# One DMA queue in order of need for the first loads, and the second layer's modulation weights moved into the first feed-forward stage

## The chip, the cores and the metric

The kernel is one program on all 8 cores of one Trainium2 chip. Each core computes one half of one of four sequences. The metric is the device time of the slowest core, in microseconds (us).

A run lists each core's span and the mean clock that TensorE (PE in the profile) was granted. Most executions agree within 0.3%, but in some of them, whatever the kernel, the cores of one die (0 to 3 or 4 to 7) or of both get a lower clock and take some per cent longer: these are slow runs. One die was also often at a lower clock than the other in runs that still count as fast, which moves the slowest core by up to 30 us. So beside the verdict of the fast runs I give, for each kernel, its **undisturbed time**: the median span over the four cores of a die, and of these the median over the dies that ran at that kernel's best clock. It is a time of middling cores, so it is lower than the time of the slowest core, and it is only compared with other undisturbed times of the same chip, unless said.

## The reference, cut to what matters

Two layers; each has a mixing sub-layer (one projection feeds a gated convolution, a spatial gate and a pooling) and a feed-forward sub-layer. Both are scaled and shifted by a modulation that is computed from a conditioning vector:

```python
for l in range(DEPTH):                                   # DEPTH = 2, D_MODEL = 1024
    ada = (c_act @ w_ada[l] + b_ada[l])[:, None, :]      # w_ada[l]: 1024 x 6144
    sh1, sc1, gt1, sh2, sc2, gt2 = jnp.split(ada, 6, axis=-1)
    h = x * (1.0 + sc1) + sh1
    z = h @ w_in[l] + b_in[l]                            # branches b, c, x, u, v, p, gates
    ...                                                  # mixers A, B, C, gates, merge, w_o
    x = layer_norm(ALPHA * x + gt1 * (merged @ w_o[l]), ...)
    h = x * (1.0 + sc2) + sh2
    up_a, up_g = jnp.split(h @ w_up[l] + b_up[l], 2, axis=-1)
    f = gelu(causal_dwconv(up_a, ...) + ...) * up_g
    x = layer_norm(ALPHA * x + gt2 * (f @ w_down[l]), ...)
```

So nothing of layer 0 can start before the first third of its modulation and x are there, and the modulation of layer 1 is not needed before layer 1.

## The kernel before

The program is recorded as a list of operations; a list scheduler with a cost model then fixes the order on every engine when the kernel is built. Weights are float32 in memory and are cast to bfloat16 on the way in, by DMAs of the GpSimd queue. They land in a pool of buffers chosen at recording time (`wget` takes one, `wput` gives it back). A core handles its 2240 tokens in two passes, each of three pieces.

Modulation weights, 512 output columns at a time, are "wada": 2.1 MB read, 32 matmuls with one column. Twelve of them make a layer.

```python
def load_x(a, b, base, dst=None, after=()):
    dst = xT[:, :, xc(base, a, b)] if dst is None else dst
    dma("sp", dst, xs[:, :, a:b], writes=[dst], nbytes=..., after=after)

def ada_step(l, g, reg=REG_W):
    h, w = wget(wada_d[l, g], 4 * UNIT, reg=reg)
    ...
    group([(P[:, jj:jj + 1], wv[:, k, jj * 128:(jj + 1) * 128], cact[:, k:k + 1], ...) for jj in range(4) for k in range(8)])
    wput(h)

def tick(n=1):                       # the next modulation step of the to-do list
    for _ in range(n):
        if todo:
            todo.pop(0)()
```

The start, and the to-do list (8 steps of layer 0, then the 12 of layer 1):

```python
load_x(*x_in[0], 0)
for g in range(4):
    ada_step(0, g, (REG_B, REG_C)[g // 2])
    if g == 2:
        hold = [R.last["pe"]]
der_mix(0)
make_h0(*x_in[0], 0)
for xp in x_in[1:]:
    load_x(*xp, 0, after=hold)
    make_h0(*xp, 0)
load_x(0, XOFF, 0, dst=stage, after=hold)
...
for g in range(4, 12):
    todo.append(must(lambda g=g: ada_step(0, g, REG_B)))
for g in range(12):
    todo.append(lambda g=g: ada_step(1, g))
```

The mixing sub-layer: eight units of mixer A (`mix_a`: three projections of 8 matmuls, so 24 matmuls for each of three token pieces), the v blocks of the spatial gate, the u part, bands, eight merges. The bias rows bcv and bsb are its side loads.

```python
def side_loads():
    dma("sp", bcv[:], rows_d[l], ..., after=[R.last["pe"]])
    dma("sp", bsb[:], bsb_d[l], ..., after=[R.last["pe"]])
    ...                                        # first time: spatial weights, bands, by GpSimd
for c in range(8):
    mix_a(c)
    if c == 0:
        side_loads()
        wv += [wget(wv_d[l, hf], 4 * UNIT, reg=REG_M) for hf in range(2)]
    tick()
    for _ in range(2 if c == 0 else 1):
        if vb: v_block(vb.pop(0))
...
for g in range(8):
    u_part(g)
    tick()
...
for j in range(8):
    merge(j)
    tick()
```

The feed-forward sub-layer runs 22 up steps, each followed by a `tick()`, then the down projection.

Of the kernel before, what the change touches and what calls it, by code (L numbers as in the profile page):

```python
# [25 lines left out]
XOFF = 64  # L26
# [5 lines left out]
UNIT = 1024  # L32
# [362 lines left out]
def record(nc, es, place):  # L395

    if True:
        def din(name, shape):
            return nc.dram_tensor(name, list(shape), F32, kind="ExternalInput").ap()

        xs = din("xs", [128, 8, TOK_IN])
# [3 lines left out]
        rows_d = din("rows", [DEPTH, 128, D])  # L405
        bsb_d = din("bsb", [DEPTH, 128, 8, 128])
# [4 lines left out]
        wmixa_d = din("wmixa", [DEPTH, 8, 128, 3 * UNIT])  # L411
# [10 lines left out]
        def sb(name, shape, dt):  # L422
            return es.enter_context(nc.sbuf_tensor(name, list(shape), dt))
# [30 lines left out]
        bcv = sb("bcv", [128, D], F32)  # L454
        bsb = sb("bsb_s", [128, 8, 128], F32)
# [20 lines left out]
        R = Prog()  # L476
# [20 lines left out]
        def act_op(out, in_, func, bias=0.0, scale=1.0, late=0.0):  # L497
            aps = [a for a in (bias, scale) if not isinstance(a, float)]
            R.add("act", [lambda e: e.activation(out=out, in_=in_, func=func, bias=bias, scale=scale)],  # L499
                  reads=[in_] + aps, writes=[out], cost=210 + 85 * len(aps) + nfree(out) / 1.2,  # L500
                  table=TBL.get(func), late=late)
# [5 lines left out]
        def ts(out, in0, s1, op0, s2=None, op1=None, eng="dve", late=0.0):  # L507
            rd = [in0] + [a for a in (s1, s2) if a is not None and not isinstance(a, float)]
            r = 1.042 if isps(in0) or isps(out) else 0.55
            c = (220 + r * nfree(out)) if eng == "dve" else 600  # L510
            if op1 is None:
                R.add(eng, [lambda e: e.tensor_scalar(out=out, in0=in0, scalar1=s1, scalar2=None, op0=op0)],
                      reads=rd, writes=[out], cost=c, late=late)
            else:
                R.add(eng, [lambda e: e.tensor_scalar(out=out, in0=in0, scalar1=s1, scalar2=s2, op0=op0, op1=op1)],  # L515
                      reads=rd, writes=[out], cost=c, late=late)
# [13 lines left out]
        def dma(eng, out, in_, reads=(), writes=(), nbytes=0, after=()):  # L530
            op = R.add(eng, [lambda e: e.dma_start(out=out, in_=in_, max_dma_last_dim=4096)], reads=reads,  # L531
                       writes=writes, cost=900 if eng == "pool" else 60, dma=True, nbytes=nbytes)
            op.deps.update(a.idx for a in after)
# [15 lines left out]
        def bank():  # L549
            i = banks.get()  # L550
            return i, PS[:, i, :]

        def proj(P, lhs, rhs, n, late=0.0):
            nk = len(lhs)
            group([(P[:, 0:n], lhs[k], rhs[k], k == 0, k == nk - 1) for k in range(nk)], late=late)
# [5 lines left out]
        def wget(src, n, at=None, reg=REG_W):  # L561

            k = n // QU
            if at is None:
                i = units.get(k, reg[0], reg[1], UNIT // QU)
            else:
                i = units.get(k, at, at + k, 1)
            dst = mem[:, i * QU:i * QU + n]
            dma("pool", dst, src, writes=[dst], nbytes=128 * n * 4)
            return (i, k), dst  # L570
# [16 lines left out]
        def xc(base, a, b):  # L587

            o = base if base else XOFF
            return slice(a - o, b - o)  # L590

        def load_x(a, b, base, dst=None, after=()):
            dst = xT[:, :, xc(base, a, b)] if dst is None else dst
            dma("sp", dst, xs[:, :, a:b], writes=[dst], nbytes=128 * 8 * (b - a) * 4, after=after)

        def make_h0(a, b, base, src=None):
            src = xT[:, :, xc(base, a, b)] if src is None else src
            for c in range(8):
                o, x = hT[:, c, LEAD + a - base:LEAD + b - base], src[:, c, :]
                bi, sc = der[:, 0, 1, c:c + 1], der[:, 0, 0, c:c + 1]  # L600
                if c % 2:
                    ts(o, x, sc, ALU.mult, bi, ALU.add)
                else:
                    act_op(o, x, AF.Identity, bias=bi, scale=sc)
# [46 lines left out]
        def tick(n=1):  # L651
# [4 lines that stand above are left out]
        def hx(k, base, a, b):  # L656
            return hT[:, k, LEAD + a - base:LEAD + b - base]
# [56 lines left out]
        def mixing(l, base, subs, blocks, zblocks, first):  # L714
            cp(hT[:, :, 0:LEAD], hcar[:, l, 0, :, :]) if not first else None
            cp(hcar[:, l, 0, :, :], hT[:, :, TMAX:TMAX + LEAD]) if first else None
            def side_loads():
                dma("sp", bcv[:], rows_d[l], writes=[bcv[:]], nbytes=128 * 4096, after=[R.last["pe"]])
                dma("sp", bsb[:], bsb_d[l], writes=[bsb[:]], nbytes=128 * 4096, after=[R.last["pe"]])
                if first and l == 0:  # L720
                    for q in range(DEPTH):
                        dma("pool", wsT[:, q].rearrange("p b c -> p (b c)"), wsT_d[:, q * 1024:(q + 1) * 1024],
                            writes=[wsT[:, q]], nbytes=128 * 4096)
                        z = wsT[64:128, q, :, 0:64]
                        R.add("dve", [lambda e, z=z: e.memset(z, 0.0)], writes=[wsT[:, q]], cost=700)
                    dma("pool", bandg[:].rearrange("p a c -> p (a c)"), bandg_d, writes=[bandg[:]], nbytes=128 * 2304)
                    dma("pool", bandf[:].rearrange("p a c -> p (a c)"), bandf_d, writes=[bandf[:]], nbytes=128 * 2304)
# [1 line left out]
            wv = []  # L729

            def mix_a(c):
                h, w = wget(wmixa_d[l, c], 3 * UNIT)
                w = w.rearrange("p (r k n) -> p r k n", r=3, k=8)
                for a, b in subs:
                    n = b - a
                    ix, Px = bank()
                    proj(Px, [w[:, 2, k, :] for k in range(8)], [hx(k, base, a - 2, b) for k in range(8)], n + 2)
                    ic, Pc = bank()
                    proj(Pc, [w[:, 1, k, :] for k in range(8)], [hx(k, base, a - 2, b) for k in range(8)], n + 2)
                    ip, pr = tmp()  # L740
                    pr = pr[:, 0:n + 2]
                    act_op(pr, Px[:, 0:n + 2], AF.Identity, bias=V(l, V_BIN + 16 + c))
                    banks.put(ix)
                    stt(pr, Pc[:, 0:n + 2], V(l, V_BIN + 8 + c), pr, ALU.add, ALU.mult)
                    banks.put(ic)
                    m0, m1 = max(a - 2, HALO - 2), min(b, HALO)
                    if first and m0 < m1:
                        z = pr[:, m0 - a + 2:m1 - a + 2]
                        ts(z, z, mask[:, 0:1], ALU.mult)
                    ib, Pb = bank()  # L750
                    proj(Pb, [w[:, 0, k, :] for k in range(8)], [hx(k, base, a, b) for k in range(8)], n)
                    iv, cv = tmp()
                    cv = cv[:, 0:n]
                    act_op(cv, pr[:, 2:n + 2], AF.Identity, scale=V(l, V_CONVA + 16 + c))
                    stt(cv, pr[:, 1:n + 1], V(l, V_CONVA + 8 + c), cv, ALU.mult, ALU.add)
                    stt(cv, pr[:, 0:n], V(l, V_CONVA + c), cv, ALU.mult, ALU.add)
                    tpool.put(ip)
                    stt(preA[:, c, xc(base, a, b)], Pb[:, 0:n], V(l, V_BIN + c), cv, ALU.add, ALU.mult)
                    banks.put(ib)
                    tpool.put(iv)  # L760
                wput(h)
# [43 lines left out]
            for hh in range(2):  # L805
                i, P = bank()
                group([(P[:, 0:512], ones[:], wsT[:, l, 4 * hh:4 * hh + 4, :].rearrange("p a b -> p (a b)"), True, True)])
                for gg in range(4):
                    g = 4 * hh + gg
# [60 lines left out]
            zb = list(zblocks)  # L870
            for g in range(8):
                u_part(g)
                tick()
                for _ in range(2 if g == 0 else 1):
                    if zb:
                        z_block(zb.pop(0))
# [67 lines left out]
            cp(pcar[:, l, :], tokz[:, zblocks[-1] - base // 128, :]) if first else None  # L944
            for j in range(8):
                merge(j)
                tick()
            wput(hp)
            while todo and getattr(todo[0], "must", False):
                tick()  # L950
# [86 lines left out]
        stage = gvs[:, 0, 0:8 * XOFF].rearrange("p (c t) -> p c t", c=8)  # L1037
        for g in range(4):
            ada_step(0, g, (REG_B, REG_C)[g // 2])
            if g == 2:  # L1040
                hold = [R.last["pe"]]
        der_mix(0)
        make_h0(*x_in[0], 0)
        for xp in x_in[1:]:
            load_x(*xp, 0, after=hold)
            make_h0(*xp, 0)
        load_x(0, XOFF, 0, dst=stage, after=hold)
        make_h0(0, XOFF, 0, src=stage)
        der_const(0)
        der_const(1)  # L1050
# [192 lines left out]
```

## Time and profile before

| | before |
|---|---|
| median of the first 3 runs | 2666.0 us (2662.22 to 2691.5) |
| median of 5 runs, with those of the comparison | 2666.26 us (2662.22 to 3013.88, one slow) |
| cores of the profiled run | 2647.5 to 2662.0 us |
| PE busy | 2497.3 us, 94% |

The prediction shows the slices, the start and the chain. Two views more. First, windows of the slowest core, core 7: the stretch in us, then for PE, PEld, DVE, ACT and POOL the busy time with the instructions in brackets, then the granted clock, the DMA share and GB/s.

```profile
60.00:80.00 20.00, 8.08 (x34) 4.00 (x33) 4.61 (x10) 3.70 (x6) 0.00 (x0) 0.67 1.07 190
280.00:320.00 40.00, 27.14 (x269) 19.14 (x267) 6.07 (x13) 12.74 (x33) 1.91 (x3) 0.74 0.64 99
```

At the start PE works 8 of 20 us, DMA is full (a share of 1.07). In the merges PE works 27 of 40 us although DMA is at 0.64: there data are late because of what stands before them in the queue and in the buffers. Both stretches run at about 0.7 of the clock. Second, the PE matmul groups of the same core over the whole span: busy time, mean ns, then the idle time just before them and what ended it.

```profile
L540 PE MATMUL PS<-hT,mem 128*128 128x384 bf16 (+9 forms) x9600 | 1511.1, 313 | 63.3 <-ACT hT L499 23.1 <-DVE hcar L524 21.4 <-DMA mem<-wmrg 12.7
L540 PE MATMUL PS<-mem 128*128 128x384 bf16 (+5 forms) x4608 | 734.9, 312 | 12.5 <-DMA mem<-wmrg 9.8 <-DVE xT L520 2.0 <-ACT tmps L499 0.6
L540 PE MATMUL PS<-mem,hT 128*128 128x512 bf16 (+1 forms) x1136 | 263.9, 386 | 16.5 <-DVE gvs L504 9.3 <-DMA mem<-wv 4.6 <-ACT hT L499 2.6
```

These three groups carry 92 us of PE's idle time. "ACT hT" is mostly x that came late (20.7 of the 23.1 us lie in the first 90 us): hT is made from x. Of "DVE hcar", the columns that one token piece hands to the next, 7.6 us are the late last piece of x at 89.95 us; the other two waits, 6.83 and 6.93 us, stand at the starts of the feed-forward stages at 536.8 and 1154.0 us, beside the layer norms, and have nothing to do with x loads. "wmrg" are the merge weights. "DVE gvs" is v work that waits for its bias row.

### The profile page before, as it was taken

To read this page: it belongs to the slowest core of one execution; us is meant where nothing else is said; L and a number is where in the kernel's file an instruction comes from. 1 tells how busy PE (TensorE), PEld (TensorE's weight loads), DVE (VectorE), ACT (ScalarE), POOL (GpSimd) and SP (SyncE) were. 2 spreads that over 40 slices of the span, in tenths; PEclk is the share of its full clock that TensorE was granted. 3 is DMA by queue.
4 is the path that set the end of the run, shared out by engine and by line. 5 is a ranking of instruction groups with operands and counts; after the bars stand their busy time and mean duration, and the time that the engine had idled before them with its cause. 6 is when DMAs were issued, how large, how long until landed. Compare 5 with 4: busy or idle time off the path is not lost.

```text
span 2662.0 us, 42484 instructions; the slowest of 8 cores (2647.5 to 2662.0 us)
## 1 busy us (share of the span) xinstructions
PE 2497.3 (94%) x17240; PEld 1592.5 (60%) x17240; DVE 1494.9 (56%) x2791; ACT 1010.0 (38%) x1848; POOL 248.4 (9%) x367
## 2 busy tenths in 40 slices
PE   2699788899999999989998999999999999999997
PEld 1365555566656566656764566656666656666665
DVE  1474233777557534577656634477646753458645
ACT  1233322554343332454532342255435333237423
POOL 1011011100000010110000100111000101011000
PEclk9899899999999999999999999999999999999999
DMA  9975666543462444644567333454326334464431
GB/s 178 164 115 93 98 102 110 97 65 50 70 115 42 75 75 73 100 77 67 116 119 162 52 59 62 73 90 80 60 44 115 53 48 70 78 100 80 72 56 64
DMA packets 131788, 227.26 MB, mean 85 GB/s; under 512 B 8080, under 2 KB 45200, under 8 KB 131600
## 3 DMA queue, kind: packets, MB, share of 16 engines
q0 software_dynamic: 107136, 197.97, 46.6%
q1 hardware_dynamic: 24464, 26.57, 3.5%
q8 instruction: 144, 2.36, 0.4%
q14 instruction: 44, 0.36, 0.0%
HBM read 414.07 MB, written 8.40 MB: 159 GB/s over the span
## 4 chain that ended last, share of the span: by engine, by line
PE 84%; DMA 8%; DVE 5%; ACT 1%; issue 1%; another core or an unknown queue 0%; POOL 0%; SPq 0%; DVEq 0%; POOLq 0%
PE PS L540 84%; DMA mem<-wmrg 2%; DVE xT L504 2%; DMA mem<-wada 2%; DMA xT<-xs 2%; DMA bcv<-rows 1%; DVE xT L520 1%; DMA y<-xT 1%; ACT hT L499 1%; DVE rsb L504 0%; DVE xT L515 0%; DVE tmps L504 0%; ACT tmps L499 0%; DVE tmps L520 0%
## 5 line engine op out<-in xcount | busy, mean ns | idle before, releaser
L540 PE MATMUL PS<-hT,mem 128*128 128x384 bf16 (+9 forms) x9600 | 1511.1, 313 | 63.3 <-ACT hT L499 23.1
L540 PEld LDWEIGHTS PS<-hT,mem 128*128 128x128 bf16 x9600 | 935.8, 98 | 570.2 <-issue 80.7
L540 PE MATMUL PS<-mem 128*128 128x384 bf16 (+5 forms) x4608 | 734.9, 312 | 12.5 <-DMA mem<-wmrg 9.8
L540 PEld LDWEIGHTS PS<-mem 128*128 128x128 bf16 x4608 | 451.0, 98 | 245.8 <-issue 15.1
L520 DVE SCALAR_TENSOR_TENSOR tmps<-PS,vecs_s,tmps 128x384 f32<-128x384 f32 (+7 forms) x624 | 357.2, 575 | 197.5 <-ACT tmps L499 163.0
L520 DVE SCALAR_TENSOR_TENSOR tmps<-tmps,PS 128x384 f32<-128x384 f32 (+4 forms) x288 | 148.7, 517 | 407.6 <-PE PS L540 298.9
L499 ACT ACTIVATE tmps<-PS,hgb 128x384 f32<-128x384 f32 (+4 forms) x288 | 159.4, 554 | 473.3 <-PE PS L540 473.3
L540 PE MATMUL PS<-mem,hT 128*128 128x512 bf16 (+1 forms) x1136 | 263.9, 386 | 16.5 <-DVE gvs L504 9.3
L499 ACT ACTIVATE tmps<-PS,cfb,vecs_s 128x384 f32<-128x384 f32 (+4 forms) x264 | 167.9, 638 | 260.3 <-PE PS L540 260.0
L520 DVE SCALAR_TENSOR_TENSOR mem<-PS,vecs_s,tmps 128x384 bf16<-128x384 f32 (+4 forms) x360 | 205.8, 574 | 22.7 <-ACT tmps L499 20.5
L520 DVE SCALAR_TENSOR_TENSOR xT<-PS,der,xT 128x384 f32<-128x384 f32 (+5 forms) x192 | 107.4, 576 | 182.9 <-PE PS L540 182.3
L540 PEld LDWEIGHTS PS<-mem,hT 128*128 128x128 bf16 (+1 forms) x1136 | 110.4, 100 | 142.7 <-issue 27.0
L499 ACT ACTIVATE tmps<-PS,vecs_s 128x384 f32<-128x384 f32 (+8 forms) x192 | 105.7, 551 | 159.9 <-PE PS L540 159.8
L499 ACT ACTIVATE tmps<-tmps 128x384 f32<-128x384 f32 (+5 forms) x288 | 139.1, 484 | 58.7 <-DVE tmps L520 58.1
L499 ACT ACTIVATE sqb<-xT 128x768 bf16<-128x768 f32 (+5 forms) x96 | 73.4, 778 | 205.6 <-DVE xT L520 205.4
L504 DVE TENSOR_TENSOR xT<-xT,tmps 128x1536 f32<-128x1536 f32 (+5 forms) x96 | 148.3, 1600 | 0.0
L520 DVE SCALAR_TENSOR_TENSOR tmps<-tmps,vecs_s 128x384 f32<-128x384 f32 (+4 forms) x192 | 110.5, 578 | 39.1 <-ACT tmps L499 36.4
L499 ACT ACTIVATE hT<-xT,der 128x384 bf16<-128x384 f32 (+5 forms) x156 | 91.4, 667 | 90.8 <-DVE der L524 37.0
L520 DVE SCALAR_TENSOR_TENSOR tmps<-PS,vecs_s,bsb_s 128x384 f32<-128x384 f32 (+4 forms) x120 | 58.4, 504 | 116.5 <-PE PS L540 115.5
L499 ACT ACTIVATE mem<-PS 128x512 bf16<-128x512 f32 (+3 forms) x168 | 76.8, 562 | 99.8 <-PE PS L540 99.8
L531 POOL DMA_DIRECT2D mem<-wup x88 | 61.9, 709 | 451.2 <-PE PS L540 438.0
L531 POOL DMA_DIRECT2D mem<-wmrg x64 | 46.8, 731 | 547.7 <-PE PS L540 547.5
(77 smaller groups left out, 1073.6 us busy)
## 6 DMA issues: line engine op xcount, KB each, us to landing
mem<-wup POOLq DMA_DIRECT2D x88, 512.0 KB, 6.6
mem<-wada POOLq DMA_DIRECT2D x24, 1024.0 KB, 13.7
mem<-wmixa POOLq DMA_DIRECT2D x32, 768.0 KB, 10.8
mem<-wmrg POOLq DMA_DIRECT2D x32, 768.0 KB, 8.7
mem<-wdn POOLq DMA_DIRECT2D x32, 704.0 KB, 7.4
mem<-wmrg POOLq DMA_DIRECT2D x32, 512.0 KB, 5.7
mem<-wv POOLq DMA_DIRECT2D x8, 1024.0 KB, 18.9
mem<-wu POOLq DMA_DIRECT2D x32, 256.0 KB, 5.2
```

The lines of the kernel that those rows point to most:

```text
L499: R.add("act", [lambda e: e.activation(out=out, in_=in_, func=func, bias=bias, scale=scale)], reads=[in_] + aps, writes=[out], cost=210 + ...
L504: R.add(eng, [lambda e: e.tensor_tensor(out=out, in0=in0, in1=in1, op=op)], reads=[in0, in1], writes=[out], cost=(165 + 1.042 * nfree(out) ...
L520: R.add("dve", [lambda e: e.scalar_tensor_tensor(out=out, in0=in0, scalar=scalar, in1=in1, op0=op0, op1=op1)], reads=rd, writes=[out], cos ...
L531: op = R.add(eng, [lambda e: e.dma_start(out=out, in_=in_, max_dma_last_dim=4096)], reads=reads, writes=writes, cost=900 if eng == "pool" ...
L540: fns.append(lambda e, o=o, l=l, r=r, st=st, sp=sp: e.matmul(o, l, r, start=st, stop=sp))
```

## The change

The intent: send everything that the start needs through one queue in the order in which it is needed, start nothing there that nobody needs yet, and keep the twelve loads of layer 1's modulation out of a stage whose own weights are tight. They move to the first feed-forward stage, whose up steps had a `tick()` already. Third, later bias loads wait for their buffer only, no longer for PE's last work. The diff, cut of its context:

```diff
-        def load_x(a, b, base, dst=None, after=()):
+        def load_x(a, b, base, dst=None, eng="sp"):
-            dma("sp", dst, xs[:, :, a:b], writes=[dst], nbytes=..., after=after)
+            dma(eng, dst, xs[:, :, a:b], writes=[dst], nbytes=...)
...
             def side_loads():
-                dma("sp", bcv[:], rows_d[l], writes=[bcv[:]], nbytes=128 * 4096, after=[R.last["pe"]])
-                dma("sp", bsb[:], bsb_d[l], writes=[bsb[:]], nbytes=128 * 4096, after=[R.last["pe"]])
+                q = "pool" if first and l == 0 else "sp"
+                dma(q, bcv[:], rows_d[l], writes=[bcv[:]], nbytes=128 * 4096)
+                dma(q, bsb[:], bsb_d[l], writes=[bsb[:]], nbytes=128 * 4096)
...
             def mix_a(c):
-                h, w = wget(wmixa_d[l, c], 3 * UNIT)
+                h, w = early.pop(0) if early else wget(wmixa_d[l, c], 3 * UNIT)
...
                 u_part(g)
-                tick()
...
                 merge(j)
-                tick()
...
             ada_step(0, g, (REG_B, REG_C)[g // 2])
-            if g == 2:
-                hold = [R.last["pe"]]
         der_mix(0)
         make_h0(*x_in[0], 0)
+        early = [wget(wmixa_d[0, 0], 3 * UNIT)]
         for xp in x_in[1:]:
-            load_x(*xp, 0, after=hold)
+            load_x(*xp, 0, eng="pool")
             make_h0(*xp, 0)
-        load_x(0, XOFF, 0, dst=stage, after=hold)
+        early.append(wget(wmixa_d[0, 1], 3 * UNIT))
+        load_x(0, XOFF, 0, dst=stage, eng="pool")
```

More of the change, by code (lines that the diff above doesn't have):

```diff
@@ L590, in xc @@
             return slice(a - o, b - o)
-        def load_x(a, b, base, dst=None, after=()):
+        def load_x(a, b, base, dst=None, eng="sp"):
             dst = xT[:, :, xc(base, a, b)] if dst is None else dst
-            dma("sp", dst, xs[:, :, a:b], writes=[dst], nbytes=128 * 8 * (b - a) * 4, after=after)
+            dma(eng, dst, xs[:, :, a:b], writes=[dst], nbytes=128 * 8 * (b - a) * 4)
         def make_h0(a, b, base, src=None):
```

## The prediction

> **What bounds the kernel now.** I read the page's forty slices first, then the timeline of the PE rows from the start, then the chain of work that ended last.
>
> Page, part 2: busy tenths in 40 slices of 66.6 us.
>
> ```profile
> PE   2699788899999999989998999999999999999997
> PEclk9899899999999999999999999999999999999999
> DMA  9975666543462444644567333454326334464431
> ```
>
> TensorE (PE) is the bound: 2497.3 us busy of a span of 2662.0, so 165 us idle. The idle time is not spread out: slices 1, 2 and 5 to 8 (up to about 530 us) are weak, the rest is full. DMA is at 9 only in slices 1 and 2. So only the first mixing sub-layer is short of data; later, data come early.
>
> PE rows from the start: start us, duration, what, and in brackets the idle time before it and what ended that.
>
> ```profile
> 16.04 0.99 PE L540 MATMUL PS<-cact,mem 128*128 128x1 bf16 x32 [16.04 <-DMA mem<-wada]
> 38.93 0.99 PE L540 MATMUL PS<-cact,mem 128*128 128x1 bf16 x32 [5.44 <-DMA mem<-wada]
> 45.09 4.72 PE L540 MATMUL PS<-hT,mem 128*128 128x276 bf16 x24 [5.17 <-DMA mem<-wmixa]
> 59.41 5.50 PE L540 MATMUL PS<-hT,mem 128*128 128x386 bf16 x24 [8.74 <-ACT hT L499]
> 77.04 5.31 PE L540 MATMUL PS<-hT,mem 128*128 128x386 bf16 x16 [11.92 <-ACT hT L499]
> 89.95 2.72 PE L540 MATMUL PS<-hT,mem 128*128 128x384 bf16 x8 [7.60 <-DVE hcar L524]
> 102.63 2.94 PE L540 MATMUL PS<-mem,hT 128*128 128x512 bf16 x8 [4.53 <-DVE gvs L504]
> ```
>
> With the two middle modulation steps, the gaps up to 102.6 us sum to 73.9 us. The first four modulation weights (wada) come in a row; then the first mixing unit waits for its weights, and its three token pieces wait for x (59.4, 77.0) and, through VectorE's order, for the last piece of x (89.95). x lies in the SP queue beside a full GpSimd queue: its second piece is issued at 34 us and lands after 22 us, the third lands 40 us after its issue, and the last quarter megabyte only at 88.3 us. The bias row bcv is issued only at 92.7 us, after PE's last work, and v starts in earnest at 102.6.
>
> The merges of the same sub-layer, same columns:
>
> ```profile
> 292.44 0.99 PE L540 MATMUL PS<-cact,mem 128*128 128x1 bf16 x32 [5.93 <-DMA mem<-wada]
> 305.87 7.01 PE L540 MATMUL PS<-hT,mem 128*128 128x274 bf16 x32 [6.67 <-DMA mem<-wmrg]
> 361.95 6.30 PE L540 MATMUL PS<-mem 128*128 128x274 bf16 x32 [4.54 <-DMA mem<-wmrg]
> 425.10 8.42 PE L540 MATMUL PS<-hT,mem 128*128 128x274 bf16 x40 [3.01 <-DMA mem<-wmrg]
> ```
>
> A layer-1 wada (2.1 MB read) sits between merge weights, in their buffer and in their queue; PE waits for both. From 103 to 500 us such gaps sum to 31.6 us. The matmuls after a gap are slow too: 32 of 274 columns took 7.01 us at 305.87, where a warm group of 8 takes 0.93.
>
> The chain of work that ended last (start, us, what), further on:
>
> ```profile
> 784.87 168.78 PE PS L540 x1101
> 957.90 157.72 PE PS L540 x1112
> ...
> 1396.14 24.50 DMA bcv<-rows
> ```
>
> The same mixing work in layer 1, without wada, runs unbroken. And once more a bias load is late: at the second pass it is issued at 1396, behind a store of y and a load of x in the SP queue; PE loses 4.81 us at 1421.58.
>
> **What the Trainium skill says.** "DMA: Bandwidth & Descriptors", section "Issuing engines are not separate DMA queues": queues of SP and GpSimd run on the same 16 engines and interleave. The trace agrees: moving x gains no bandwidth; bytes read (float32, twice what a cast writes) per time between landings (issue time plus time to landing) were about the same, 0.31 to 0.32 MB/us, in every stretch from 54 to 108 us, with x in flight or not. Same page, "Queues, rings and completion order": each engine takes turns between queue rows by packets. The trace agrees that this makes the small SP transfers late (0.26 MB landing 14 us after the piece before). One queue in the order of need is thus the right cure. "TensorE: Matmul & The Clock Gate", part 1: an idle array drops to half clock and needs about 3.4 us of work to come back. The trace shows the cost: a granted clock of 0.67 from 60 to 80 us, 0.74 from 280 to 320, and 1.00 in unbroken stretches. Closing gaps pays more than the gaps.
>
> **The change, part by part.** The built order of the changed kernel shows: GpSimd queue: 4 wada, mixing weights 0, x pieces 2 and 3, mixing weights 1, last x piece, bcv, bsb, spatial weights, bands, two wv, then wada 5, mixing weights 2 and 3, and so on. No instruction is added or removed on TensorE; 12 modulation groups move from the u and merge loops into the first FFN.
>
> (1) Start. wada 4 lands about 1 us before its old 38.8; mixing weights 0, without x beside them (0.75 MB at 0.32 MB/us), at 42.5 instead of 44.9. Then at 0.32 MB/us: x pieces 3.15 MB to 52.3; mixing weights 1 (1.57) 57.2; last x piece 59 (2 us, my allowance for its 256-byte rows); bcv and bsb (1.05) 62.5; spatial weights and bands (1.64 MB at the 0.238 MB/us they had before) 69.4; wv halves 76.0 and 82.6. So v can run in full from T = 83 us. By then PE has done units 0 and 1 (10.64 us each when warm), the ones product (1.4) and, by the built order, 4 half blocks of v (6.9): 29.6 us. Before, at 102.6, it had done one unit, the ones product and 3 half blocks: 17.3. The head start is 20 + 12 = 32 us.
>
> (2) The rest of the mixing. Warm, as layer 1 has it: 8 units and 18 v halves at 1.727, 8 modulation groups at 0.80, ones: 124; u part as 888.6 to 951.1 plus 18 more tokens: 62.9; bands 8; merges to the FFN start as 958.7 to 1154.0 plus the tokens: 198.3. Sum 393.2; less 29.6 leaves 363.6 after T. Against it, new waits: the 8 wada of layer 0 still come in this stage, now with less time before them. Sending wada (6.6 us each) and mixing weights (4.9) through the queue from T on and PE's groups in their built order beside it, I find seven waits of 0.7 to 2.4 us, about 10 us. FFN start: 83 + 364 + 10 = 457, against 536.8 before: 80 us earlier. (Check from the other side: 32 us head start, 31.6 of gaps gone, about 16 of slow-clock matmuls gone (102.6 to 536.8 took 434.2, of which 385.6 is warm work counted as above and 33 are gaps), plus 12 modulation groups x 0.80 = 9.6 moved out, less 10 of new waits: 79.)
>
> (3) First FFN. The 9.6 us come back. Data: per step of 10.64 + 0.80 us, one up-weight (1.05 MB) and one wada (2.1): 3.15 MB in 11.4 us is 0.275 MB/us, below 0.32. By the built waits a wada may start about three steps (some 32 us) before its use; going through the queue, each lands over 15 us early. Cost 0 to 3 us, taken as 1.
>
> (4) Side loads. They no longer wait for PE's last work but for the buffer alone; the second pass's bcv moves ahead of the stores of y. That gives back the 4.8 us, perhaps 1 more from wv, which has less beside it: 5.5.
>
> Sum: -80 + 9.6 + 1 - 5.5 = -75; from 2666 to about 2591 us.
>
> **Rivals.** (a) Supply stays the bound at the start: the order changes, not the bytes. For it: DMA full to 108 us, and from T the 8 wada and 6 mixing weights want 85 us of queue for 94 us of PE work. If the one queue runs at 0.28 instead of 0.32, T becomes 89 and the new waits double: about 2608. (b) The x pieces are slow in the shared queue: rows of 1.5 KB and 256 bytes, where wada has 4 KB pieces; the skill's DMA page ("Specifications") asks for 512 bytes or more for line rate, and no trace here isolates it. If the last piece takes 14 us as it did beside others, everything behind it slips 12: about 2603. (c) The wada waits move along into the FFN: 12 at the 2.6 us of a typical wait in the mixing give 31 back: about 2621, within 2%. Against it: layer-0 wada with about that slack (103 to 210 us) cost no wait in the kernel before. (d) The order around the layer norms changes by the scheduler; some 10 us of gaps lie at each such place: either way 5 us.
>
> **Range and chances.** Centre 2590. Most errors push up ((a) to (c)), few down (the 10 us of new waits not appearing, more clock won): 2572 to 2615. 2% is 2613; (a) or (b) alone stays below it, (c) or two together do not. Faster 0.85, same 0.14, slower 0.01.
>
> **What would show it.** Right: in the changed profile PE waits for x end by 56 us, wv half two lands at 80 to 87 us, the FFN's first full group starts at 450 to 465, no wait for wmrg, granted clock near 1 from 90 to 450, waits for wada below 15 us in all after 45 us, no bcv wait near 1350. Wrong: v starting after 92 us (a, b); gaps before modulation groups in the FFN (c); or a gain of the start that is lost again before 450 us in waits for wada or mixing weights.

## The result, and the profile after

| | before | after |
|---|---|---|
| median of 5 runs | 2666.26 us | 2583.65 us |
| lowest and highest | 2662.22, 3013.88 | 2580.74, 2819.17 |
| cores of the profiled run | 2647.5 to 2662.0 us | 2570.9 to 2582.0 us |
| PE busy | 2497.3 us, 94% | 2482.8 us, 96% |

Each kernel had one slow run of the five. The ratio of the fast runs is 0.9674, with a 95% interval of 0.9612 to 0.9736: faster by 3.3%. Ratios in this document are the mean time of one kernel's fast runs over that of the other's of the same rounds, so not quite the ratio of the medians.

The slices of the changed kernel's page, in the order of those in the prediction:

```profile
PE   3999999999999999999999999999999999999997
PEclk9999999999999999999999999999999999999999
DMA  9983447895444344544493244544507324464432
```

Slices 2 and 5 to 8 of PE, which were at 6 to 8, are full. DMA, which was at 6 in slices 5 to 7, is at 4 in slices 5 and 6 and now peaks in slices 7 to 9, just before and in the first part of the feed-forward stage: the moved loads.

PE rows from the start of its slowest core, core 5, as in the prediction:

```profile
38.52 0.99 PE L540 MATMUL PS<-cact,mem 128*128 128x1 bf16 x32 [5.69 <-DMA mem<-wada]
42.81 5.47 PE L540 MATMUL PS<-hT,mem 128*128 128x276 bf16 x24 [3.30 <-ACT hT L499]
50.86 20.31 PE L540 MATMUL PS<-hT,mem 128*128 128x386 bf16 x120 [2.57 <-ACT hT L499]
...
73.78 12.25 PE L540 MATMUL PS<-mem,hT 128*128 128x512 bf16 x56 [1.53 <-DVE bsb_s L520]
86.42 0.94 PE L540 MATMUL PS<-cact,mem 128*128 128x1 bf16 x32 [0.40 <-DMA mem<-wada]
...
91.67 15.29 PE L540 MATMUL PS<-hT,mem 128*128 128x276 bf16 x96 [2.56 <-DVE stat L783]
```

The only wait for x after the first piece is the 2.57 us at 50.86; from there two mixing units run in one piece. In the old kernel the waits for x were 8.74, 11.92 and 7.60 us. The v blocks start at 73.8. The old kernel's core 5 started them at 92.7, did three half blocks and waited 4.56 us for bcv before the fourth.

The windows and the PE groups of core 5, columns as above:

```profile
60.00:80.00 20.00, 18.47 (x110) 10.44 (x108) 14.56 (x31) 6.94 (x12) 1.51 (x2) 1.00 1.08 170
280.00:320.00 40.00, 40.00 (x276) 26.54 (x274) 17.74 (x34) 10.59 (x20) 2.94 (x4) 1.00 0.52 77
```

```profile
L540 PE MATMUL PS<-hT,mem 128*128 128x384 bf16 (+9 forms) x9600 | 1514.0, 313 | 21.1 <-ACT hT L499 8.1 <-DVE tmps L520 5.0 <-DVE stat L783 2.6
L540 PE MATMUL PS<-mem 128*128 128x384 bf16 (+5 forms) x4608 | 735.4, 311 | 0.0
L540 PE MATMUL PS<-mem,hT 128*128 128x512 bf16 (+1 forms) x1136 | 256.7, 379 | 5.0 <-DMA mem<-wv 2.3 <-DVE bsb_s L520 1.5 <-ACT hT L499 1.1
```

The matmul counts are the same; the idle time before these groups fell from 92.3 us to 26.1. The wait for merge weights is gone from every row. Some 11 us of the fall are the two hcar waits beside the norms (now 1.25 and 1.00 us), but new waits of 1.98 and 5.0 us stand beside them: the scheduler ordered that work differently and gained 4 to 5 us by it, which none of the three parts below accounts for. At the start DMA is as full as before (1.08 against 1.07), and PE does more than twice the work under it: the bytes are the same, their order is not. The granted clock is 1.00 in both stretches.

The first feed-forward stage, two of its up steps and the one wait:

```profile
504.58 7.23 PE L540 MATMUL PS<-hT,mem 128*128 128x274 bf16 x48
...
512.46 7.23 PE L540 MATMUL PS<-hT,mem 128*128 128x274 bf16 x48
...
555.30 0.94 PE L540 MATMUL PS<-cact,mem 128*128 128x1 bf16 x32 [4.12 <-DMA mem<-wada]
```

A step with its modulation group takes 512.46 - 504.58 = 7.9 us, and the last of the twelve modulation loads comes 4.12 us late (0.9 to 4.7 us on the eight cores). The chain that ended last names the supply in the same places:

```profile
5.35 42.72 DMA xT<-xs
...
89.18 33.40 DMA mem<-wada
...
528.69 26.37 DMA mem<-wada
```

Where the time went, on core 5 of both profiles, from the same marks in the PE timeline (core 7 in brackets):

| mark | before | after | gained up to here |
|---|---|---|---|
| first v block | 92.7 | 73.8 | 18.9 (19.2) |
| u part | 213.1 | 184.4 | 28.7 (29.5) |
| first feed-forward group | 530.1 | 461.0 | 69.1 (77.8) |
| v of layer 1 | 776.7 | 714.8 | 61.9 (67.9) |
| u of layer 1 | 884.2 | 817.8 | 66.4 (72.6) |
| v of the second pass | 1401.0 | 1329.7 | 71.3 (75.2) |
| u of the second pass | 1516.3 | 1434.9 | 81.4 (83.9) |
| end of PE | 2645.7 | 2568.2 | 77.4 (80.8) |

The rows do not all stand at the same work, because the order of the matmuls was rebuilt. Counted in the built programs, the changed kernel has done 72 matmuls more than the old one at its first v block (10.6 us at the traces' rates), 40 feed-forward matmuls and two modulation groups more at its first feed-forward group (5.4 + 1.6 us), and 24 matmuls more at the v of layer 1 (2.6 us); at the three u rows the two agree to within one matmul. Corrected for that, some 76 us are gained up to the feed-forward stage on core 5 (85 on core 7), the stage with its twelve modulation groups gives back 12 (14), and after it 13 (10) more come in.

### The profile page after: what moved, and what is told of

It reads as the page before. It is cut to its first block, busy times and chain, and to the rows that moved or that the text cites. A ratio compares the mean times of both kernels' runs of the same rounds, so it can differ in the third digit from the quotient of the medians.

```text
span 2582.0 us, 42469 instructions; the slowest of 8 cores (2570.9 to 2582.0 us)
## 1 busy us (share of the span) xinstructions
PE 2482.8 (96%) x17240; PEld 1588.6 (62%) x17240; DVE 1498.1 (58%) x2791; ACT 1016.1 (39%) x1850; POOL 253.2 (10%) x372
## 4 chain that ended last, share of the span: by engine, by line
PE 86%; DMA 7%; DVE 4%; ACT 2%; issue 1%; POOL 0%; DVEq 0%; POOLq 0%
PE PS L540 86%; DMA mem<-wada 3%; DVE xT L504 2%; DMA xT<-xs 2%; DMA mem<-wv 1%; ACT hT L499 1%; DVE xT L520 1%; DMA bsb_s<-bsb 0%; ACT tmps L499 0%; DMA gvs<-xs 0%; DVE tmps L520 0%; ACT L499 0%; DVE rsb L504 0%; POOL mem L531 0%; DVE tmps L504 0%
## 5 line engine op out<-in xcount | busy, mean ns | idle before, releaser
L540 PE MATMUL PS<-mem,hT 128*128 128x512 bf16 (+1 forms) x1136 | 256.7, 379 | 5.0 <-DMA mem<-wv 2.3
L531 POOL DMA_DIRECT2D mem<-wup x88 | 61.9, 708 | 384.3 <-PE PS L540 345.0
## 6 DMA issues: line engine op xcount, KB each, us to landing
mem<-wv POOLq DMA_DIRECT2D x8, 1024.0 KB, 17.9
```

The source lines that it names most:

```text
L531: op = R.add(eng, [lambda e: e.dma_start(out=out, in_=in_, max_dma_last_dim=4096)], reads=reads, writes=writes, cost=900 if eng == "pool" ...
L540: fns.append(lambda e, o=o, l=l, r=r, st=st, sp=sp: e.matmul(o, l, r, start=st, stop=sp))
```

## The experiments

All kernels are built anew for each run, so most edits also change the order of instructions. Comparing the built programs: extra_u and extra_fix keep the order of PE, ScalarE and VectorE of the changed kernel; in the other variants it differs, so what they gain or lose includes an unknown share of the order. By the 2% rule s_only, t_only and b_only are "same" as before, x_sp and extra_start "unclear", the rest faster; the smaller effects rest on the undisturbed times and the traces.

My theory: three separate gains. (S) At the start the supply of bytes sets the pace, and order of need lets PE work under it. (T) Layer-1 modulation weights delay the merges' own weights, and their gaps slow the clock; in the feed-forward stage they cost little. (B) Late bias loads cost a few us per pass. The rivals: one part does nearly everything; moving x to the GpSimd queue is what counts, not the order; or the start is paced by engines, not by bytes.

| run | change | median | fast-run ratio to before | undisturbed | to its neighbour |
|---|---|---|---|---|---|
| chip A: before | | 2665.76 | | 2651.9 | |
| s_only | start alone | 2641.6 | 0.9867 | 2614.4 | -37 to before |
| t_only | modulation move alone | 2654.11 | 0.9929 | 2626.1 | -26 to before |
| b_only | later bias loads alone | 2654.2 | 0.9928 | 2633.8 | -18 to before |
| x_sp | all, x left in the SP queue | 2613.89 | 0.9785 | 2587.4 | +12 to the whole change of chip B |
| chip B: before | | 2665.77 | | 2655.5 | |
| full_again | the whole change | 2585.05 | 0.9716 | 2575.8 | -80 to before |
| extra_start | + 2.1 MB unread, at the start | 2734.01 | 1.0173 | 2693.2 | +117 to full_again |
| extra_u | + 2.1 MB unread, in the u part | 2582.13 | 0.9687 | 2573.1 | -3 to full_again |
| uspread | 3 modulation loads earlier | 2604.33 | 0.9752 | 2573.4 | -2 to full_again |
| chip C: before | | 2662.27 | | 2651.5 | |
| full_ref | the whole change | 2581.89 | 0.9702 | 2572.7 | -79 to before |
| extra_fix | + 2.1 MB unread, order of all engines kept | 2646.58 | 0.9727 | 2580.6 | +8 to full_ref |
| best | v weights first, loads spread | 2625.57 | 0.9673 | 2564.4 | -8 to full_ref |

The medians are over all runs, slow ones too: for extra_fix 5 of 8 and for best 4 of 6 were slow, so their medians say nothing about the kernels. All eleven gave correct results.

**s_only: the start alone.** The changed kernel with the ticks back in the u part and the merges, and the later bias loads held as before:

```diff
                 u_part(g)
+                tick()
...
                 merge(j)
+                tick()
...
+                hold = [] if first and l == 0 else [R.last["pe"]]
-                dma(q, bcv[:], rows_d[l], writes=[bcv[:]], nbytes=128 * 4096)
+                dma(q, bcv[:], rows_d[l], writes=[bcv[:]], nbytes=128 * 4096, after=hold)     # bsb likewise
```

> Start part alone (x pieces, first bias row and table in the GpSimd queue in order of need, first mixing weights ahead; all modulation loads and the later bias loads as before). My theory, that the parts add up: the spatial part begins about 29 us earlier as in the full change, the waits between the merges stay (28 to 33 us of gaps up to the first FFN), so about 2666 - 30 = 2636 us (2628 to 2645). Rival, that supply only moves the wait on: what is won at the start is lost to new waits for modulation and mixing weights before the merges, so 2655 or more.

Fast runs: 0.9867 (0.982 to 0.9915); undisturbed 37 us better. The u part starts 26 to 32 us earlier on the eight cores, much as in the whole change. Between it and the feed-forward stage PE still waits 20 to 30 us for merge and modulation weights (before: 21 to 31; in t_only and in the whole change no core waits for them there at all). One such row, core 1:

```profile
273.77 5.70 PE L540 MATMUL PS<-hT,mem 128*128 128x274 bf16 x32 [9.07 <-DMA mem<-wmrg]
```

So the start's gain is kept to the end without the rest, and it does not cure the merges: here 32 matmuls that read hT waited 9.07 us for merge weights. Not all of the 37 us is the start, though: on cores 1 and 2 27 to 30 us are there by the u part of layer 1, and 7 come in up to the u part of the second pass, which the edit does not aim at; the rebuilt order may have done that.

**t_only: the modulation move alone.** The old kernel less two lines:

```diff
                 u_part(g)
-                tick()
...
                 merge(j)
-                tick()
```

> Modulation of layer 1 moved into the first FFN, nothing else. My theory: gaps before merge weights go (about 30 us) and with them some 10 us of slow-clock matmuls; 10 us of modulation matmuls only move; a wait of some 4 us comes up in the FFN: about 2666 - 35 = 2631 us (2622 to 2640), granted clock near 1 in the merges. Rival: waits move along with the loads into the FFN, 2650 or more. If start and modulation add up, the savings of this run and of the start alone sum to 60 to 70.

Fast runs: 0.9929 (0.9883 to 0.9976); undisturbed 26 us better, less than expected. Windows of core 1 from 285 to 320 us, the old kernel's first, t_only's second (columns as before):

```profile
285.00:320.00 35.00, 25.52 (x223) 17.58 (x224) 7.23 (x16) 7.64 (x16) 1.98 (x3) 0.77 0.58 84
```

```profile
285.00:320.00 35.00, 35.00 (x231) 22.79 (x230) 13.61 (x26) 8.85 (x16) 1.45 (x2) 0.97 0.35 58
```

The gaps are closed and the clock is up from 0.77 to 0.97, as the theory has it. But the feed-forward stage takes back more than expected. From its first group to the v blocks of layer 1 core 1 took 763.3 - 517.7 = 245.6 us before and 748.0 - 484.6 = 263.4 now: 17.9 us more, and core 2 likewise 15.2, where the moved matmuls are only 12 x 0.80 = 9.6. Two of t_only's rows there, core 1:

```profile
586.35 0.94 PE L540 MATMUL PS<-cact,mem 128*128 128x1 bf16 x32 [4.02 <-DMA mem<-wada]
...
654.73 14.57 PE L540 MATMUL PS<-mem 128*128 128x272 bf16 x110 [2.09 <-DMA mem<-wdn]
```

Of the excess, 6.1 us are these two waits: modulation weights that come late, and down weights behind them. In the whole change the same rows are only 7 to 10 us further apart, but that is mostly the marks, as said above: at equal work it is 12 to 14.

**b_only: the later bias loads alone.** The old kernel, with the hold kept only where it was needed at the start:

```diff
-                dma("sp", bcv[:], rows_d[l], ..., after=[R.last["pe"]])
+                hold = [R.last["pe"]] if first and l == 0 else []
+                dma("sp", bcv[:], rows_d[l], ..., after=hold)             # bsb likewise
```

> Only the later bias loads freed from waiting for TensorE's last work. My theory: the wait for the bias row at the second pass goes, 8 to 10 us between the second pass's start of v and its spatial part, nothing else: about 2657 us, within 1% of before. Rival: the wait for the v weights takes its place and the time stays at 2664 to 2666.

Fast runs: 0.9928 (0.9885 to 0.9971); undisturbed 18 us better, twice what was expected. The second pass, core 5, the old kernel's rows first, then b_only's:

```profile
1401.00 5.30 PE L540 MATMUL PS<-mem,hT 128*128 128x512 bf16 x16 [4.17 <-DMA mem<-wv]
...
1416.44 3.57 PE L540 MATMUL PS<-mem,hT 128*128 128x512 bf16 x8 [5.80 <-DVE gvs L504]
```

```profile
1399.26 9.77 PE L540 MATMUL PS<-mem,hT 128*128 128x512 bf16 x32 [3.99 <-DMA mem<-wv]
```

The wait for gvs, that is for bcv, is gone; on this core the one for wv stays, and PE's idle time between v and u of this pass falls from 10.0 to 4.0 us. On other cores the wait for wv goes too. Core 4, the old kernel's rows; b_only has no wait of either kind there:

```profile
1396.88 1.89 PE L540 MATMUL PS<-mem,hT 128*128 128x512 bf16 x8 [2.12 <-DMA mem<-wv]
...
1407.51 3.17 PE L540 MATMUL PS<-mem,hT 128*128 128x512 bf16 x8 [8.74 <-DVE gvs L504]
```

On cores 1, 2 and 4 the stretch from v to u takes 102 to 104 us where it took 117 to 118; 2.6 of that are two groups of matmuls that the new order puts before v. The granted clock in it goes from 0.97 to 1.00 on core 4. From the u part of layer 1 to that of the second pass, rows that stand at equal work, the gain is 15.5 to 16.0 us on these cores and 12.2 on core 5. So nearly all of the 18 lies where the bias loads of the second pass are waited for; what the order adds to it is not separated.

The three parts alone sum to -37 - 26 - 18 = -81 us; the whole change gains 79 to 80 on chips B and C. So no single part carries it, and they add up to about the whole. That the two agree to 2 us is in part luck: s_only has 7 us in the second pass that its edit does not aim at, and the waits beside the norms change by a few us with the rebuilt order.

**x_sp: everything but the queue of x.** The changed kernel with the x loads back in the SP queue, in their new place and without a hold:

```diff
-            load_x(*xp, 0, eng="pool")
+            load_x(*xp, 0)
-        load_x(0, XOFF, 0, dst=stage, eng="pool")
+        load_x(0, XOFF, 0, dst=stage)
```

> The full change, but the later x pieces go by the SP queue again, all issued in the first microseconds. Queue theory: beside a full GpSimd queue they land late (second about 50, third about 70, last after 75 us), the second mixing unit waits for the last x piece, and the head start shrinks by 8 to 14 us: about 2595 us. Rival, that only the order of the weights and the removed hold matter: within 3 us of the full change, 2581 to 2587.

Fast runs: 0.9785 (0.9746 to 0.9824); undisturbed 2587.4, which is 12 us more than the whole change on chip B and 15 more than on chip C, so a comparison across chips. Its start, core 1:

```profile
67.18 5.15 PE L540 MATMUL PS<-hT,mem 128*128 128x386 bf16 x16 [10.40 <-ACT hT L499]
78.54 10.01 PE L540 MATMUL PS<-hT,mem 128*128 128x384 bf16 x56 [6.21 <-ACT tmps L499]
```

PE waits 10.4 and 6.2 us for x again (the second by way of ScalarE, which waited 9.69 us for the last piece), and the v blocks start at 88.4 us instead of 73.8. Removing the hold is not enough: the third piece of x landed at 64.4 us and the last at 76.6, in the whole change at 52.9 and 58.9. So some 12 to 15 us of the whole change are the single queue. The traces show that x comes late there, not how the engines share their time between the two queues.

**extra_start: more bytes at the start.** If bytes set the pace there, an unread load of 2.1 MB just ahead of the v weights must delay v by about 2.1 / 0.32 = 6.6 us; if engines do, by nothing.

```diff
                 if c == 0:
                     side_loads()
+                    if first and l == 0:
+                        wput(wget(wada_d[1, 0], 4 * UNIT, reg=REG_B)[0])
                     wv += [wget(wv_d[l, hf], 4 * UNIT, reg=REG_M) for hf in range(2)]
```

> The full change with one more load of 2.1 MB that nobody reads, put just before the two v weights of the first sub-layer. Supply theory (the stretch before v is paced byte by byte): the v weights land 6 to 7 us later and the undisturbed cores end 5 to 9 us later. Rival (TensorE is 96% busy, a load more is hidden): below 2 us.

The v blocks came 6.8 us later, as the supply theory says, but the kernel became 117 us slower (rounded to 118 in a text below), which neither theory allows. Two of its rows, core 1:

```profile
104.53 0.99 PE L540 MATMUL PS<-cact,mem 128*128 128x1 bf16 x32 [15.54 <-DMA mem<-wada]
...
148.84 4.08 PE L540 MATMUL PS<-hT,mem 128*128 128x386 bf16 x24 [0.77 <-ACT tmps L499]
```

The load took a buffer that the modulation weights need, and the scheduler, which saw another cost, built another order on PE, ScalarE, VectorE and GpSimd. A mixing unit with its share of v took 20.5 us instead of 14.9, waiting for ScalarE every few groups. So the experiment changed two things, and its total proves nothing about the bytes.

**extra_u: the same bytes later.** The same unread load in the u part, where DMA is half idle:

```diff
                 u_part(g)
+                if first and l == 0 and g == 2:
+                    wput(wget(wada_d[1, 0], 4 * UNIT)[0])
```

> The same unread load of 2.1 MB, but in the spatial part of the first sub-layer, where the DMA engines are near idle. Supply theory: it is hidden there, within 2 us of the full change on undisturbed cores (the order of the merge loads changes a little). Rival, that every load in this queue costs its 6.6 us wherever it lies: 5 us or more.

Undisturbed 2.7 us less than the whole change, fast runs 0.9687 (0.9673 to 0.97): hidden. That stage has room for 2.1 MB. Only the order of the GpSimd queue changed, so this is a clean test.

**uspread: three modulation loads earlier.** As the u part has room and the feed-forward stage is short, three steps of layer 1 go back to the u part, and the feed-forward stage ticks in two of three steps:

```diff
                 u_part(g)
+                if g % 2 == 0:
+                    tick()
...
-                tick()                    # in the feed-forward up loop
+                if c % 3 != 2:
+                    tick()
```

> The full change, but three of the twelve layer-1 modulation loads go into the spatial part (every second step) and the other nine are spread in the FFN, two in three steps instead of one each step. Theory: an FFN step is 7.07 us of matmuls, so one modulation load a step asks 3.15 MB in 7.9 us, 0.40 MB per us, over the 0.32 the queue gives; spread, the wait of 4 us for modulation weights in the FFN goes to 0 to 1, and the undisturbed cores gain 3 to 7 us. Rival (the wait has to do with buffers or the order around the norm, not with the rate): the FFN still waits 3 us or more for them.

No wait for modulation weights is left in the feed-forward stage on any of the eight cores (1.4 to 4.3 us in full_again). Undisturbed it is 2.4 us better, which is less than the spread between the dies of one kernel (2574.4 to 2578.0 for full_again at its best clock): the wait is cured, a gain in time is not shown. Its fast runs, 0.9752 (0.9712 to 0.9792), look slower than the whole change's 0.9716, but in four of six runs a die ran at 0.984 to 0.986, where it ran at 0.99 in the others.

**extra_fix: the bytes again, with the order held.** The same 2.1 MB ahead of the v weights, put in after scheduling and into two buffers that nothing uses then; the order of the other instructions on all engines is the same as in the changed kernel:

```diff
+                    if first and l == 0:
+                        for d, n0, n1 in ((sqb, 0, 3 * UNIT), (rsb, 3 * UNIT, 4 * UNIT)):
+                            d = d[:].rearrange("p a b n -> p (a b n)")[:, 0:n1 - n0]
+                            dma("pool", d, wada_d[1, 0, :, n0:n1], writes=[d], nbytes=0)
+                            R.ops[-1].table = "ghost"     # kept out of the scheduling, inserted after it
```

> The unread 2.1 MB before the v weights again, but now with the order of every engine held as in the full change (they go to the norm's square buffers, idle then, and the scheduler does not see them). Supply theory: v weights land 6 to 7 us later and the undisturbed dies end 5 to 8 us later than the full change. Rival, that a load more is hidden: below 2 us. If it is 5 to 8, the 118 us that the first try cost were the work of the changed order and not of the bytes.

Core 1 (its matmul line is L546):

```profile
81.23 14.26 PE L546 MATMUL PS<-mem,hT 128*128 128x512 bf16 x56 [8.74 <-DMA mem<-wv]
```

PE waits 8.74 us for wv, v starts 4.7 to 7.5 us later on the eight cores (5.9 in the mean), and the end is 7.9 us later undisturbed (the ratios, 0.9727 against 0.9702, agree). Bytes ahead of the v weights are paid for about one to one: the supply paces the start. And of the 117 us of extra_start about 109 were the order and the buffer, not the bytes.

**best: v weights ahead of what they do not need.** As bytes pace the start, the v weights go ahead of bsb, the spatial weights and the bands; the first modulation tick comes two units later; and the loads are spread as in uspread:

```diff
                 if c == 0:
-                    side_loads()
+                    dma("pool" if first and l == 0 else "sp", bcv[:], rows_d[l], ...)
                     wv += [wget(wv_d[l, hf], 4 * UNIT, reg=REG_M) for hf in range(2)]
-                tick()
+                    side_loads()          # now without bcv
+                if c >= 2:
+                    tick()
```

> The full change, with what the runs suggest: v weights ahead of the spatial tables (2.2 MB) at the start, no modulation step beside the first two mixing units, two of layer 0's and one of layer 1's modulation steps in the spatial part, the rest at two in three FFN steps. Theory: v weights land 6 to 7 us earlier, the waits for modulation and mixing weights after 80 us (about 6 us) and in the FFN (4 us) go: undisturbed dies near 2563 us (2558 to 2570) against 2575. Rival, that the order around the products and norms eats it: within 4 us of 2575.

Core 1:

```profile
66.75 3.61 PE L540 MATMUL PS<-mem,hT 128*128 128x512 bf16 x16 [0.28 <-ACT tmps L499]
...
127.48 0.94 PE L540 MATMUL PS<-cact,mem 128*128 128x1 bf16 x32 [1.46 <-DMA mem<-wada]
```

The v blocks start at 66.8 us instead of 73.7 (with 29 matmuls fewer done before them), undisturbed 8.3 us are gained on the whole change, and the two fast runs took 2573.7 and 2573.59 us where full_ref's took 2579.0 to 2587.21. With two fast runs the ratio is 0.9673 (0.9654 to 0.9692), where full_ref has 0.9702 (0.9687 to 0.9717): the intervals overlap a little. So it is the fastest kernel, by about 0.3%; which of its edits does it was not separated.

## Why the prediction was right

The time came out at 2583.65 us, 6 below the centre of 2590 and inside the range, and the mechanism held in three of the four steps. But the sum was helped by errors of opposite sign. By its own steps, with core 5 (core 7 in brackets), corrected to equal work as below the table of marks:

**(1) Start: held.** The second half of the v weights landed at 79.9 us, predicted 82.6. Up to the last piece of x the sum was exact (58.9 us, predicted 59): its 2 us for 256-byte rows were 1.0 in the trace, but the mixing weights before it came 0.6 later. The difference came after it: the two bias loads took 2.6 us where 3.5 were allowed, the spatial weights and bands 5.5 where 6.9 were. Rival (b), 14 us for that last piece, did not appear. The waits for x ended at 50.9. That bytes pace the start was a reading of the trace then; extra_fix shows it. Rival (a) in its strong form, 0.28 MB/us, did not appear: from 42.3 to 122.6 us 25.5 MB landed, 0.32 MB/us. (For the old kernel, 17.0 MB landed from 56.6 to 108.2 us, 0.33 MB/us, a little more than the 0.31 to 0.32.)

**(2) The rest of the mixing: held.** The feed-forward stage was to start at 457, 80 us earlier; its first full group starts at 461.0 (459.0). At equal work the gain is 76 us (85). No wait for merge weights is left on any core. The new waits after T were 0.40 + 2.56 + 0.98 + 1.15 + 0.44 + 0.23 = 5.8 us, where 10 were predicted. Part of the gain is no work of the change: of rival (d), the order around the norm, the good side came: the wait of 6.83 us at the stage's start became two of 1.98 and 1.25. One reading was off without effect: the 32 matmuls of 7.01 us at 305.87 are, by the built order, 24 of 274 columns and 8 of 384, so about 4.1 us when warm, not 3.7.

**(3) The first feed-forward stage: the step that was wrong.** "Data: per step of 10.64 + 0.80 us" took the length of a mixing unit, which has 24 matmuls per piece. A feed-forward step has two projections where a unit has three, so 16 per piece: about 7.1 + 0.80 = 7.9 us in the trace. So the demand is 3.15 MB in 7.9 us = 0.40 MB/us, not 0.275, and above the 0.32 that the queue gave, not below. The three steps of lead are then 24 us, not 32, and the last load took 26.4 us from issue to landing (528.69 in the chain). "Each lands over 15 us early" was therefore false for the last one, which came 4.12 us late. The cost stayed small: the stage gave back 12 us (14), of which 10.6 were predicted. Rival (c), all twelve waiting, did not occur.

**(4) Side loads: right in kind, half the size.** 5.5 us were predicted; b_only gained 18, and in the whole change 13 us (10) came in after the feed-forward stage. The term counted one visible wait, 4.81 us on core 7. In b_only the other cores lost waits of up to 8.74 us for the bias row, the waits for the v weights beside it and the slow clock after both.

**The clock.** Predicted near 1; it is 1.00 in the windows shown, 0.67 and 0.74 before.

So in sum: (2) gained 4 less on core 5 and 5 more on core 7 than the 80, (3) cost 1 to 4 more than the 10.6, (4) gained 5 to 8 more than the 5.5. That these nearly cancel is luck.

## What to carry to other kernels

While a queue is full, order its loads by how much matmul time each opens per byte, in one queue, and let nothing that is not needed yet go first; the bytes need not change for the time to fall. Before moving bulk loads to another stage, divide the bytes of one step by that step's own measured length, not by that of a similar-looking stage. Where a scheduler fixes the order at build, hold the order when you test a cost: one unread load moved the time by 117 us when the order changed with it, and by 8 when it did not.

## What the Trainium skill lacked or had wrong

- "DMA: Bandwidth & Descriptors", "Specifications", asks for 512 bytes or more for line rate. Here a last piece of x with 256-byte rows, 0.26 MB, landed 1.0 us after the piece before it in the GpSimd queue, so near 0.26 MB/us against 0.32 for all loads there. Against 0.8 us at that rate it is some 0.2 us more; the same piece landed 12 to 14 us after the one before it in the SP queue beside a full GpSimd queue (x_sp, and the kernel before). The row size was not what made it late.
- The same page, "Queues, rings and completion order", says that engines take turns between queues by packets, but not what share a stream of small rows gets beside large ones. The trace of x_sp shows the cost of that: waits of 10.4 and 6.2 us for x, and 12 to 15 us at the end.
- No figure of that page is for loads that cast float32 to bfloat16 on all 8 cores at once. Here the start's loads, most of them casting, ran at 0.32 MB/us of bytes read per core (25.5 MB from 42.3 to 122.6 us), and 2.1 MB more cost 4.7 to 7.5 us at the v blocks.
- "TensorE: Matmul & The Clock Gate", part 1, advises to budget 13/16 of the clock for dense matmuls on all cores. That holds for the default power profile, and the record does not say which one this chip had. Here the fast runs of the changed kernel on the first chip held a granted mean of 0.99 on all 8 cores, and clocks of 0.81 to 0.89 on a die, near 13/16, came in slow runs only.
- No page has the sensitivity of a statically ordered program to one load more: 117 us with the order rebuilt, 8 with it held.
